# Where a transformer block keeps its modulation sums, which queue writes its spills, and when two modulation sections are loaded

## The chip, the cores and the metric

The kernel runs on one core of a Trainium2 chip. The core has five engines that run side by side and meet through semaphores: TensorE (PE, matmuls), VectorE (DVE), ScalarE (ACT), GpSimd (POOL) and SyncE (SP, which here only issues transfers). Matmuls write to PSUM; everything else lives in SBUF; VectorE and ScalarE can read and write both. Transfers between SBUF and the chip's main memory are issued from an engine's instruction queue and carried by 16 DMA engines. The metric is the device time in microseconds (us) of one execution; lower is better.

## The reference

One transformer block over 1024 tokens of width 1024, in float32, with adaptive layer norm:

```
mod = silu(c) @ w_ada + b_ada                     # 6 sections of 1024
sh_a, sc_a, g_a, sh_f, sc_f, g_f = split(mod, 6)  # sections 0 .. 5
h = rms_norm(x) * (1 + sc_a) + sh_a
x = x + g_a * hybrid_mixer(h, ...)                # w_in, two kinds of attention, w_out
h = rms_norm(x) * (1 + sc_f) + sh_f
x = x + g_f * swiglu(h, w_gate, w_up, w_down)
return rms_norm(x, g_final)
```

The mixer projects `h` by `w_in` (1024 x 2240) into q and k of four "differential" heads (the first 1024 columns), their values dv (512 columns), and two low-rank latents (lq 384, lk 320 columns) from which four further heads (MLA) get their q, k and v by `w_q_up` and `w_kv_up`. Both kinds of attention are causal, in blocks of 128 queries.

The six sections of `mod` are needed at different times. Sections 1 and 0 (scale and shift of the first norm) are needed before the first projection; section 2 (`g_a`) when `w_out` is prepared; 4 and 3 (scale and shift of the second norm) before the feed-forward part; 5 (`g_f`) when `w_down` is prepared, which multiplies it into the weights.

## The kernel before

**Number format.** Every float32 operand of a large matmul is split into two parts, `hi` (rounded by a ScalarE copy) and `lo = raw - hi` (a subtraction on VectorE or GpSimd). `mm3` then issues three matmuls (hi x hi, hi x lo, lo x hi; lines 370 to 372) for each product. The helper `split` does this for weights and activations, `evac` for results that leave PSUM; both subtractions are recorded under line 151.

**Buffers.** Nearly all SBUF tiles, weights, activations and temporaries alike, come from one pool of `NBUF` = 49 slots of 4 KB per partition (`slot`). An instruction that writes a fresh slot waits until the last user of that slot is done; for a tile that is spilled to main memory this last user is the transfer. PSUM has eight banks: two double-bank tiles (`psd`) and four single ones (`psb`).

**Weight streams.** `Stream` is a list of items, each with a load (`dma`) and a preparation (`prep`). `pump(n)` prepares the next n items and keeps `ahead` loads in flight beyond them, but only up to the item named by `allow`; `need(name)` pumps until that item is prepared. All loads are issued on SP's queue, in order. `st` feeds the first half of the kernel, `st2` the weights of `w_out`, gate, up and down.

**Order of the work.** The parts that bear on the change, in program order:

1. `load_ada(k)`, `ada_cols(k)`: scale and shift of the first norm for 128 columns at a time (k = 0 to 7). VectorE multiplies eight 128 x 256 pieces of `w_ada` by the entries of `silu(c)` and adds them up in `acc` (lines 222, 224, 226); TensorE adds over the partitions by four small matmuls against ones (line 229); VectorE writes the two columns `acol` (230, 232). The items `("ada", k)` alternate in `st` with `("s0", k)`, the k-th 128 rows of the q and k weights, whose `lo` part is subtracted on GpSimd.
2. `make_h(hf, k)`: TensorE transposes 128 columns of four normalised x tiles into one PSUM bank (line 356); ScalarE scales and shifts them into the SBUF tile `ht` (361); `split` makes `hh` and `hl` from it.
3. `g1(hf)`, for each half of the tokens: for k = 0 to 7, six targets times `mm3` (18 matmuls of 128 x 512), with `make_h(hf, k + 2)` prepared meanwhile; in the first half, `ada_cols` and the splits of s0 run in this loop. Then the last two targets (48 matmuls). Six targets fill the two `psd` tiles and two of the four `psb` banks. `evac_qk` moves each target into a tile `E` and, some ticks later (`defer`, `tick`), `spill` writes `E` to the scratch arrays `scr_q` and `scr_k` in main memory by two transfers of 256 KB (line 404), issued on GpSimd's queue (`sd`).
4. The dv loop: eight token tiles with 24 matmuls each, evacuated by `evac_v` and spilled by four transfers per pair of tiles (line 472), also on GpSimd's queue.
5. The list `fill`: lq, lk, q_up, kv_up, between which the first units of attention already run; `PUMP` sets how many items of `st` are prepared per entry, `ALLOW` when further items may be loaded.
6. The loop of attention units (`step`), `w_out` and the second norm, gate and up (`gu`), then down.

The other modulation sections are made by `ada_items`: eight loads of 512 KB (`adr`, line 268), each followed by a VectorE multiply-add of 128 x 1024 (lines 275, 277). When the eighth is done, `done` is deferred by three ticks. For `row_bc` (sections 2 and 5) it issues two matmuls against ones (line 299) and two additions; the result `gbc` stays in a slot until it is used. For `col_sec` (sections 4 and 3) it issues eight narrow products (line 309, recorded as 16 matmuls) and the additions into `fcol`. These matmuls are pinned: TensorE executes them where the program text puts them, waiting if the sums aren't there yet. Instructions that are not pinned may be ordered otherwise than in the text when the kernel is built.

The order of `st` before: ada/s0 alternating, x tiles 4 to 7, section 2, section 4, dv, lq, section 3, section 5, lk, rope tables, q_up, kv_up. `g1(1)` may load up to dv; the dv loop up to the end of section 5.

Of the kernel before, what the change touches and what calls it, by code (L numbers as in the profile page):

```python
# [21 lines left out]
LT = 4  # L22
PD = 1
DSP = 2
ALLOW = [(6, 'rope'), (15, ('qup', 2)), (25, ('kvup', 1)), (34, None)]
SPILL = 'gpsimd'
DS = 4
ND = 2
LA = 5
PUMP = (2, 2)  # L30
LC = 1
KEEP = [(n, (0, b)) for n in ("qn", "kn", "qp") for b in range(2)]
LEAD = 2
# [63 lines left out]
def emit(ctx, tc, a, out, dbg=None, rec=None):  # L97
# [21 lines left out]
    def psb():  # L119
        return pp.tile([P, 512], F32, name=nm("psb"), tag="b", bufs=8 - 2 * ND)  # L120
# [93 lines left out]
            ld(out=adar[k][q], in_=a["ada_a"][k, :, q * 4:(q + 1) * 4, :])  # L214

    def ada_cols(k):
        acc = slot([2, 256], F32, "acc")
        for kt in range(8):
            src = adar[k][kt // 4][:, kt % 4, :]
            c = cact[:, kt:kt + 1]  # L220
            if kt < 2:
                nc.vector.tensor_scalar(out=acc[:, kt, :], in0=src, scalar1=c, scalar2=None, op0=ALU.mult)
            else:
                nc.vector.scalar_tensor_tensor(out=acc[:, kt % 2, :], in0=src, scalar=c, in1=acc[:, kt % 2, :],
                                               op0=ALU.mult, op1=ALU.add)
        nc.vector.tensor_tensor(out=acc[:, 0, :], in0=acc[:, 0, :], in1=acc[:, 1, :], op=ALU.add)
        ps = psb()
        for s in range(2):
            mm(ps[:, s:s + 1], lhsT=acc[:, 0, s * 128:(s + 1) * 128], rhs=ones[:, 0:1], start=True, stop=True)
        nc.vector.scalar_tensor_tensor(out=acol[:, 0, k:k + 1], in0=ps[:, 0:1], scalar=b1col(1, k),  # L230
                                       in1=V[:, 56 + k:57 + k], op0=ALU.add, op1=ALU.mult)
        nc.vector.tensor_tensor(out=acol[:, 1, k:k + 1], in0=ps[:, 1:2], in1=bcol(0, k), op=ALU.add)
        del adar[k]
# [3 lines left out]
    def witem(st, name, src, shape, eng=None, split_=None, view=None):  # L237
        def dma():
            raws[name] = slot(shape, F32, "raw")
            ld(out=raws[name], in_=src)  # L240

        def prep():
            hi = slot(shape, F32R, "whi")
            lo = slot(shape, F32R, "wlo")
            split(raws[name], hi, lo, eng)
            W[name] = (hi, lo)
            del raws[name]

        st.add(name, dma, prep)
# [5 lines left out]
    win = a["w_in"]  # L255
    for k in range(8):
        st.add(("ada", k), (lambda k=k: load_ada(k)) if k else (lambda: None), lambda k=k: ada_cols(k))
        witem(st, ("s0", k), win[k * P:(k + 1) * P, 0:1024], [1024], nc.gpsimd)
    for t in range(4, 8):
        st.add(("x", t), lambda t=t: load_x(t), lambda t=t: x_norm(t))  # L260

    accs = {}

    def ada_items(sec, done):
        for kt in range(8):
            def dma(kt=kt):
                raws[("ad", sec, kt)] = slot([1024], F32, "adr")
                ld(out=raws[("ad", sec, kt)], in_=a["w_ada"][kt * P:(kt + 1) * P, sec * 1024:(sec + 1) * 1024])

            def prep(kt=kt):  # L270
                src = raws.pop(("ad", sec, kt))
                c = cact[:, kt:kt + 1]
                if kt == 0:
                    accs[sec] = slot([1024], F32, "acc")
                    nc.vector.tensor_scalar(out=accs[sec], in0=src, scalar1=c, scalar2=None, op0=ALU.mult)
                else:
                    nc.vector.scalar_tensor_tensor(out=accs[sec], in0=src, scalar=c, in1=accs[sec],
                                                   op0=ALU.mult, op1=ALU.add)
                if kt == 7:
                    acc = accs.pop(sec)  # L280
                    defer(3, lambda: done(acc))

            st.add(("ad", sec, kt), dma, prep)

    gbc = {}

    def row_bc(sec):
        def dma():
            raws[("gb", sec)] = slot([1024], F32, "gbr")
            ld(out=raws[("gb", sec)], in_=a["b_ada"][0:1, sec * 1024:(sec + 1) * 1024].to_broadcast([P, 1024]))  # L290

        st.add(("gb", sec), dma, lambda: None)

        def done(acc):
            g = slot([1024], F32, "gbc")
            br = raws.pop(("gb", sec))
            for n in range(2):
                ps = psb()
                pin(mm(ps, lhsT=ones, rhs=acc[:, n * 512:(n + 1) * 512], start=True, stop=True))
                nc.vector.tensor_tensor(out=g[:, n * 512:(n + 1) * 512], in0=ps, in1=br[:, n * 512:(n + 1) * 512], op=ALU.add)  # L300
            gbc[sec] = g

        ada_items(sec, done)

    def col_sec(sec, fin):
        def done(acc):
            ps = psb()
            for j in range(8):
                pin(mm(ps[:, j:j + 1], lhsT=acc[:, j * 128:(j + 1) * 128], rhs=ones[:, 0:1], start=True, stop=True))
            fin(ps)  # L310

        ada_items(sec, done)

    def fin_scf(ps):
        nc.vector.tensor_tensor(out=fcol[:, 0, :], in0=ps[:, 0:8], in1=V1[:, 32:40], op=ALU.add)
# [2 lines left out]
    def fin_shf(ps):  # L318
        nc.vector.tensor_tensor(out=fcol[:, 1, :], in0=ps[:, 0:8], in1=V[:, 32:40], op=ALU.add)

    row_bc(2)
    col_sec(4, fin_scf)
    for q in range(4):
        witem(st, ("dv", q), win[q * 256:(q + 1) * 256, 1024:1536].rearrange("(k p) n -> p k n", p=P), [2, 512], nc.gpsimd)
    for q in range(4):
        witem(st, ("lq", q), win[q * 256:(q + 1) * 256, 1536:1920].rearrange("(k p) n -> p k n", p=P), [2, 384])
    col_sec(3, fin_shf)
    row_bc(5)

    def load_tabs():  # L330
        raws["rope"] = slot([8, 2, 64], F32, "rope")
        ld(out=raws["rope"], in_=a["rope"])

    for q in range(3):
        n = 3 if q < 2 else 2
        witem(st, ("lk", q), win[q * 384:q * 384 + n * 128, 1920:2240].rearrange("(k p) n -> p k n", p=P), [n, 320])
# [2 lines left out]
        witem(st, ("qup", k), a["w_q_up"][k * P:(k + 1) * P, :], [768], nc.gpsimd)  # L339
    for k in range(2):  # L340
        witem(st, ("kvup", k), a["w_kv_up"][k * P:(k + 1) * P, :], [1024], nc.gpsimd)


    def x_norm(t):
# [8 lines left out]
    def make_h(hf, k):  # L353
        ps = psb()
        for t in range(4):
            nc.tensor.transpose(ps[:, t * 128:(t + 1) * 128], xr[hf * 4 + t][:, k * 128:(k + 1) * 128], ident)
        if k % 2 == 0:
            hT[hf, k // 2] = (slot([2, 512], F32R, "hh"), slot([2, 512], F32R, "hl"))
        hi, lo = (z[:, k % 2, :] for z in hT[hf, k // 2])
        tmp = slot([512], F32, "ht")  # L360
        nc.scalar.activation(tmp, ps, AF.Identity, scale=acol[:, 0, k:k + 1], bias=acol[:, 1, k:k + 1])
        split(tmp, hi, lo)

    def h_op(hf, k):
        hi, lo = hT[hf, k // 2]
# [30 lines left out]
    def evac_qk(ps, m, hf):  # L396
        E = slot([2, 512], F32R, "E")
        h = m % 4
        evac(ps, -0.125 / SLOPES[h] if m < 4 else 1.0, E[:, 0, :], E[:, 1, :])

        def spill():
            q = scr["q" if m < 4 else "k"][h, hf].rearrange("(l r) m t -> l m r t", l=2)
            for l in range(2):
                sd(out=q[l], in_=f(E[:, l, :]))

        defer(DS, spill)

# [44 lines left out]
    st.allow(("dv", 3))  # L452
    g1(1)
    st.need(("dv", 3))
    st.allow(("ad", 5, 7))


    vt = {}
# [1 line left out]
    def evac_v(ps, name, t):  # L460
        if t % 2 == 0:
            vt[name] = (slot([2, 512], F32R, "vh"), slot([2, 512], F32R, "vl"))
        hi, lo = vt[name]
        evac(ps, 1.0, hi[:, t % 2, :], lo[:, t % 2, :])
        if t % 2 == 0:
            return

        def spill():
            for l, z in ((0, hi), (1, lo)):
                for tt in range(2):  # L470
                    u = t - 1 + tt
                    sd(out=scr[name][:, u // 4, :, l, u % 4, :].rearrange("h p d -> p h d"),
                       in_=f(z[:, tt, :]).rearrange("p (h d) -> p h d", h=4))

        defer(DS, spill)
# [225 lines left out]
    NP = NF // 2  # L701
    KINDS = ("gate", "up")
    scratch("g", [NF, P, 1024])
    for c in range(NP):
        its = [it for kind in KINDS for it in ops_items(kind, c)]
        for z in IT0 if c == 0 else range(8):
            st2.add(*its[z])
    for fi in range(NF):
        down_item(fi)
        g_item(fi)  # L710
# [574 lines left out]
```

## Time and profile before

| | before |
|---|---|
| median of 3 runs (lowest to highest) | 1356.33 us (1353.53 to 1357.04) |
| the profiled execution | 1355.32 us |
| its span, first to last instruction | 1353.5 us |
| mean granted TensorE clock | 0.965 |
| TensorE matmuls busy | 1245.5 us, 92% of the span |
| VectorE busy | 843.7 us, 62% |
| GpSimd busy | 534.8 us, 40% |
| ScalarE busy | 454.7 us, 34% |
| bytes moved by DMA | 180.61 MB |

In the rows of the profile an instruction is named by its line, engine, operation and tiles ("out<-in"); numbers of buffers are left out, so that `hl<-ht,hh` stands for every subtraction that makes an `hl`. A matmul's record is longer than the time after which the next one starts: matmuls overlap, and the rate is read from how many start in a stretch. "[9.24 <-DVE hl L151]" behind a row means that the engine was idle for 9.24 us before it and what ended that. Rows of waits give the engine that waited, what it waited for, the total, the times and the longest. Rows of transfers give what is issued, from which queue, how often, the size of one and the median time from issue to landing; those of queues, packets, MB and the share of the 16 DMA engines. `PEclk` is the clock that TensorE was granted, 1.00 being the full one.

### The profile page before, as it was taken

What the parts mean: (1) busy time and instruction counts of PE and PEld (TensorE: products, weight loads), DVE (VectorE), ACT (ScalarE), POOL (GpSimd) and SP (SyncE); (2) the same over time, 40 slices, a digit from 0 to 9 for tenths busy, and PEclk for the clock granted to TensorE, in tenths of its full rate; (3) what the DMA queues carried; (4) which work ended last, traced back from release to release, by engine and by line L of the source; (5) the groups of instructions that cost most, each with busy time, mean ns of one, the idle gap of its engine ahead of it and who ended that gap; (6) DMA issues with size and microseconds to landing.
All of it is one profiled execution on the core that took longest, in us unless ns stands there. A gap on an engine that the chain in (4) does not pass through costs nothing.

```text
span 1353.5 us, 16478 instructions
## 1 busy us (share of the span) xinstructions
PE 1245.5 (92%) x6033; PEld 1041.0 (77%) x6033; DVE 843.7 (62%) x1219; ACT 454.7 (34%) x801; POOL 534.8 (40%) x576
## 2 busy tenths in 40 slices
PE   4795995999999999999889999999999988999996
PEld 3574774898888898887668888888888866887885
DVE  6762426165778887867875545565555689576446
ACT  3241220254566676314632232322232332121002
POOL 3341421236564335412474444455544563221003
PEclk9897896999999999999999999999999989999998
DMA  9537589433687533441021222222221764231003
GB/s 365 198 73 192 184 189 330 141 118 98 214 293 255 172 114 108 154 140 62 32 84 57 94 94 87 84 88 85 93 70 55 247 267 134 68 125 47 0 0 124
DMA packets 66765, 180.61 MB, mean 133 GB/s; under 512 B 20654, under 2 KB 23036, under 8 KB 66556
## 3 DMA queue, kind: packets, MB, share of 16 engines
q1 hardware_dynamic: 40891, 139.58, 30.0%
q0 software_dynamic: 25792, 39.97, 10.1%
q8 instruction: 48, 0.79, 0.2%
q14 instruction: 34, 0.27, 0.1%
HBM read 135.37 MB, written 44.04 MB: 133 GB/s over the span
## 4 chain that ended last, share of the span: by engine, by line
PE 70%; DVE 11%; DMA 7%; issue 5%; ACT 4%; POOL 2%; SPq 0%; POOLq 0%; DVEq 0%; ACTq 0%
PE psb L370 14%; PE psb L371 14%; PE psb L372 14%; PE psd L371 6%; PE psd L370 5%; PE psd L372 5%; PE psb L829 2%; DMA adr<-in_w_ada_dram 2%; DMA scr_q<-E 2%; DMA scr_k<-E 1%; DVE x L1175 1%; DVE wlo L151 1%; PE psb L853 1%; PE psb L854 1%; PE psb L852 1%
## 5 line engine op out<-in xcount | busy, mean ns | idle before, releaser
L371 PE MATMUL psb<-al,whi 128*128 128x512 f32 x528 | 206.8, 392 | 3.5 <-DVE al L151 3.5
L370 PE MATMUL psb<-ah,whi 128*128 128x512 f32 x528 | 206.6, 391 | 0.2 <-ACT ht L1057 0.2
L372 PE MATMUL psb<-ah,wlo 128*128 128x512 f32 x528 | 206.2, 391 | 0.0
L1175 DVE TENSOR_TENSOR x<-psd,x 128x1024 f32<-128x1024 f32 x87 | 105.8, 1220 | 77.5 <-PE psd L372 77.5
L370 PE MATMUL psd<-dhi,whi 128*128 128x512 f32 x348 | 138.1, 397 | 13.0 <-DVE x L1175 12.9
L371 PE MATMUL psd<-dlo,whi 128*128 128x512 f32 x348 | 136.8, 393 | 0.0
L372 PE MATMUL psd<-dhi,wlo 128*128 128x512 f32 x348 | 136.8, 393 | 0.0
L1134 DVE TENSOR_TENSOR cf<-psb,uv 128x512 f32<-128x512 f32 x88 | 60.4, 686 | 115.7 <-PE psb L372 115.1
L1141 POOL TENSOR_TENSOR cf<-cf,cf 128x512 f32<-128x512 f32 x44 | 61.7, 1402 | 178.9 <-DVE cf L1134 173.6
L371 PEld LDWEIGHTS psb<-al,whi 128*128 128x128 f32 x528 | 99.5, 188 | 25.2 <-DVE al L151 4.7
L370 PEld LDWEIGHTS psb<-ah,whi 128*128 128x128 f32 x528 | 99.7, 189 | 21.7 <-ACT ht L1057 0.7
L372 PEld LDWEIGHTS psb<-ah,wlo 128*128 128x128 f32 x528 | 99.6, 189 | 20.8
L639 POOL TENSOR_TENSOR raw<-raw,gbc 128x1024 f32<-128x1024 f32 x26 | 66.9, 2587 | 102.9 <-DVE x L1175 48.8
L151 DVE TENSOR_TENSOR wlo<-raw,whi 128x1024 fp32r<-128x1024 f32 (+3 forms) x51 | 92.7, 1823 | 6.4 <-ACT whi L155 5.0
L155 ACT CAST whi<-ssum 128x1024 fp32r<-128x1024 f32 x44 | 45.0, 1044 | 136.2 <-POOL ssum L151 136.2
L370 PEld LDWEIGHTS psd<-dhi,whi 128*128 128x128 f32 x348 | 66.0, 190 | 30.8 <-DVE x L1175 17.2
L151 DVE TENSOR_TENSOR wlo<-ssum,whi 128x1024 fp32r<-128x1024 f32 x44 | 62.9, 1430 | 39.5 <-ACT whi L155 39.5
L748 ACT ACTIVATE s<-s,nb 128x640 f32<-128x640 f32 (+7 forms) x96 | 74.5, 778 | 34.0 <-DVE nb L746 30.6
L746 DVE CUSTOM_DVE_ANT_0 s<-psd,tabs 128x640 f32<-128x640 f32 (+7 forms) x80 | 63.4, 804 | 32.2 <-PE psd L772 30.3
L155 ACT CAST whi<-raw 128x1024 fp32r<-128x1024 f32 (+3 forms) x68 | 68.5, 1019 | 41.9 <-DVE dlo L151 29.9
L372 PEld LDWEIGHTS psd<-dhi,wlo 128*128 128x128 f32 x348 | 66.0, 190 | 14.2 <-DVE wlo L151 0.3
L371 PEld LDWEIGHTS psd<-dlo,whi 128*128 128x128 f32 x348 | 66.2, 190 | 13.6
(290 smaller groups left out, 2958.5 us busy)
## 6 DMA issues: line engine op xcount, KB each, us to landing
adr<-in_w_ada_dram SPq DMA_DIRECT2D x32, 512.0 KB, 10.5
raw<-in_w_gate_dram SPq DMA_DIRECT2D x22, 512.0 KB, 4.4
raw<-in_w_up_dram SPq DMA_DIRECT2D x22, 512.0 KB, 3.4
scr_g<-cf POOLq DMA_DIRECT2D x22, 512.0 KB, 4.4
raw<-in_w_down_dram SPq DMA_DIRECT2D x22, 512.0 KB, 4.3
raw<-scr_g SPq DMA_DIRECT2D x22, 512.0 KB, 4.6
ada<-in_ada_a_dram SPq DMA_DIRECT2D x16, 512.0 KB, 10.2
x<-in_x_dram SPq DMA_DIRECT2D x16, 512.0 KB, 5.1
```

The lines of the kernel that those rows point to most:

```text
L151: eng.tensor_tensor(out=o, in0=x, in1=y, op=ALU.subtract)
L155: nc.scalar.copy(hi, raw)
L370: mm(o, lhsT=ah, rhs=bh, start=start, stop=False)
L371: mm(o, lhsT=ah, rhs=bl, start=False, stop=False)
L372: mm(o, lhsT=al, rhs=bh, start=False, stop=stop)
L639: eng.tensor_tensor(out=r, in0=r, in1=gbc[sec], op=ALU.mult)
L746: nc.vector.tensor_tensor_reduce(out=s, in0=src, in1=tab, op0=ALU.add, op1=ALU.min, scale=scale, scalar=3.0e38, accum_out=nb[:, m:m + 1])
L748: nc.scalar.activation(s, s, AF.Exp, bias=nb[:, m:m + 1], scale=-1.0, accum_out=rs[:, m:m + 1])
L829: nc.tensor.transpose(ps[:, z * 128:(z + 1) * 128], p[:, kb * 128:(kb + 1) * 128], ident)
L1134: nc.vector.tensor_tensor(out=o, in0=x, in1=y, op=ALU.add)
L1141: nc.gpsimd.tensor_tensor(out=g, in0=g, in1=o, op=ALU.mult)
L1175: nc.vector.tensor_tensor(out=r, in0=d.rearrange("p a b -> p (a b)"), in1=r, op=ALU.add)
```

## The change

Four things are changed.

- `ada_cols` takes a PSUM bank at its start and keeps its two running sums in it; only the eighth product goes to an SBUF tile, to which the other sum is added. The column sums then go to the same bank.
- `make_h` writes the scaled and shifted block back to the PSUM bank of the transposes; the slot `ht` goes. The `lo` part of `s0,0` is subtracted on VectorE.
- The spills of q, k and dv are issued on ScalarE's queue, those of the MLA heads stay on GpSimd's.
- Section 3 leaves `st` for a stream `st3` that is pumped once per attention step after the list `fill`; section 5 joins `st2`, two items behind each gate/up pair from the second on, and a `tick` is added to the gate/up loop; section 4 goes behind dv, its load of `b_ada` (`gb`) of section 2 two items later. The limits are set anew: the dv loop may load up to lk, `ALLOW` has three entries, `PUMP` is one item per entry.

```diff
-ALLOW = [(6, 'rope'), (15, ('qup', 2)), (25, ('kvup', 1)), (34, None)]
+ALLOW = [(0, 'rope'), (12, ('qup', 2)), (25, None)]
-PUMP = (2, 2)
+PUMP = (1, 1)
     def ada_cols(k):
-        acc = slot([2, 256], F32, "acc")
+        ps = psb()
+        part = [ps[:, 0:256], ps[:, 256:512]]
+        acc = slot([256], F32, "acc")
         for kt in range(8):
             src = adar[k][kt // 4][:, kt % 4, :]
             c = cact[:, kt:kt + 1]
             if kt < 2:
-                nc.vector.tensor_scalar(out=acc[:, kt, :], in0=src, scalar1=c, ...)
+                nc.vector.tensor_scalar(out=part[kt], in0=src, scalar1=c, ...)
             else:
-                nc.vector.scalar_tensor_tensor(out=acc[:, kt % 2, :], in0=src, scalar=c, in1=acc[:, kt % 2, :],
+                nc.vector.scalar_tensor_tensor(out=acc if kt == 7 else part[kt % 2], in0=src, scalar=c, in1=part[kt % 2],
                                                op0=ALU.mult, op1=ALU.add)
-        nc.vector.tensor_tensor(out=acc[:, 0, :], in0=acc[:, 0, :], in1=acc[:, 1, :], op=ALU.add)
-        ps = psb()
+        nc.vector.tensor_tensor(out=acc, in0=acc, in1=part[0], op=ALU.add)
...
-        witem(st, ("s0", k), win[k * P:(k + 1) * P, 0:1024], [1024], nc.gpsimd)
+        witem(st, ("s0", k), win[k * P:(k + 1) * P, 0:1024], [1024], nc.gpsimd if k else nc.vector)
...
-    row_bc(2)
-    col_sec(4, fin_scf)
-    # dv, lq
-    col_sec(3, fin_shf)
-    row_bc(5)
+    for it in row_bc(2):
+        st.add(*it)
+    # dv
+    for it in col_sec(4, fin_scf):
+        st.add(*it)
+    # lq, lk, rope, qup, kvup
+    st3 = Stream(2)
+    for it in col_sec(3, fin_shf):
+        st3.add(*it)
...
-        tmp = slot([512], F32, "ht")
-        nc.scalar.activation(tmp, ps, AF.Identity, scale=acol[:, 0, k:k + 1], bias=acol[:, 1, k:k + 1])
-        split(tmp, hi, lo)
+        nc.scalar.activation(ps, ps, AF.Identity, scale=acol[:, 0, k:k + 1], bias=acol[:, 1, k:k + 1])
+        split(ps, hi, lo)
...
-                sd(out=q[l], in_=f(E[:, l, :]))
+                nc.scalar.dma_start(out=q[l], in_=f(E[:, l, :]))
...
-    st.allow(("ad", 5, 7))
+    st.allow(("lk", 2))
...
-                    sd(out=scr[name][:, u // 4, :, l, u % 4, :].rearrange("h p d -> p h d"),
+                    (nc.scalar.dma_start if name == "dv" else sd)(out=scr[name][:, u // 4, :, l, u % 4, :].rearrange("h p d -> p h d"),
...
+    late_ada = row_bc(5)
     for c in range(NP):
...
+        if c >= 1:
+            for _ in range(2):
+                if late_ada:
+                    st2.add(*late_ada.pop(0))
...
         step(n, LA)
+        if n > done:
+            st3.allow()
+            st3.pump()
...
             next(gen[w])
             more(m)
+            tick()
```

More of the change, by code (lines that the diff above doesn't have):

```diff
@@ L221, in ada_cols @@
             if kt < 2:
-                nc.vector.tensor_scalar(out=acc[:, kt, :], in0=src, scalar1=c, scalar2=None, op0=ALU.mult)
+                nc.vector.tensor_scalar(out=part[kt], in0=src, scalar1=c, scalar2=None, op0=ALU.mult)
             else:
-                nc.vector.scalar_tensor_tensor(out=acc[:, kt % 2, :], in0=src, scalar=c, in1=acc[:, kt % 2, :],
+                nc.vector.scalar_tensor_tensor(out=acc if kt == 7 else part[kt % 2], in0=src, scalar=c, in1=part[kt % 2],
                                                op0=ALU.mult, op1=ALU.add)
-        nc.vector.tensor_tensor(out=acc[:, 0, :], in0=acc[:, 0, :], in1=acc[:, 1, :], op=ALU.add)
-        ps = psb()
+        nc.vector.tensor_tensor(out=acc, in0=acc, in1=part[0], op=ALU.add)
         for s in range(2):
-            mm(ps[:, s:s + 1], lhsT=acc[:, 0, s * 128:(s + 1) * 128], rhs=ones[:, 0:1], start=True, stop=True)
+            mm(ps[:, s:s + 1], lhsT=acc[:, s * 128:(s + 1) * 128], rhs=ones[:, 0:1], start=True, stop=True)
         nc.vector.scalar_tensor_tensor(out=acol[:, 0, k:k + 1], in0=ps[:, 0:1], scalar=b1col(1, k),
@@ L264, in ada_items @@
     def ada_items(sec, done):
+        its = []
         for kt in range(8):
@@ L281, in prep @@
                     defer(3, lambda: done(acc))
-            st.add(("ad", sec, kt), dma, prep)
+            its.append((("ad", sec, kt), dma, prep))
+        return its
     gbc = {}
@@ L290, in dma @@
             ld(out=raws[("gb", sec)], in_=a["b_ada"][0:1, sec * 1024:(sec + 1) * 1024].to_broadcast([P, 1024]))
-        st.add(("gb", sec), dma, lambda: None)
         def done(acc):
@@ L301, in done @@
             gbc[sec] = g
-        ada_items(sec, done)
+        its = ada_items(sec, done)
+        return its[:6] + [(("gb", sec), dma, lambda: None)] + its[6:]
     def col_sec(sec, fin):
@@ L310, in done @@
             fin(ps)
-        ada_items(sec, done)
+        return ada_items(sec, done)
     def fin_scf(ps):
@@ L319, in fin_shf @@
         nc.vector.tensor_tensor(out=fcol[:, 1, :], in0=ps[:, 0:8], in1=V[:, 32:40], op=ALU.add)
-    row_bc(2)
-    col_sec(4, fin_scf)
[L323 to L326, printed above, removed]
-    col_sec(3, fin_shf)
-    row_bc(5)
     def load_tabs():
@@ L332, in load_tabs @@
         ld(out=raws["rope"], in_=a["rope"])
+    for it in row_bc(2):
+        st.add(*it)
+    for q in range(4):
+        witem(st, ("dv", q), win[q * 256:(q + 1) * 256, 1024:1536].rearrange("(k p) n -> p k n", p=P), [2, 512], nc.gpsimd)
+    for it in col_sec(4, fin_scf):
+        st.add(*it)
+    for q in range(4):
+        witem(st, ("lq", q), win[q * 256:(q + 1) * 256, 1536:1920].rearrange("(k p) n -> p k n", p=P), [2, 384])
     for q in range(3):
```

## The prediction

> **What bounds the kernel now.** I read the windows by stage first, then the waits of TensorE, then the engines' timelines where it waited.
>
> ```profile
> 20.00:95.30 75.30, 63.08 (x248) 48.61 (x249) 56.30 (x99) 23.93 (x37) 29.47 (x23) 0.86 0.52 184
> 95.30:171.50 76.20, 58.35 (x236) 45.88 (x235) 26.02 (x31) 18.39 (x27) 22.92 (x21) 0.82 0.67 186
> 171.50:245.20 73.70, 55.26 (x223) 44.58 (x223) 31.49 (x40) 10.43 (x17) 16.90 (x22) 0.84 0.90 273
> 420.00:580.00 160.00, 156.01 (x1031) 140.19 (x1029) 128.73 (x293) 93.79 (x208) 66.66 (x95) 1.00 0.45 145
> 700.00:1000.00 300.00, 300.00 (x1325) 248.53 (x1324) 163.75 (x173) 83.98 (x111) 152.00 (x112) 1.00 0.24 85
> ```
>
> Each row gives a stretch and its length, the busy time (and number) of TensorE's matmuls, its weight loads, VectorE, ScalarE and GpSimd, then TensorE's granted clock, the DMA share and GB/s. The first three rows are `g1(0)`, `g1(1)` and the dv loop; then attention; last, gate/up. In gate/up TensorE does 1325 matmuls in 300 us, 0.226 us each, never idle, at full clock. The first three stages each hold 192 matmuls of that width, 43.4 us of work, and take 74 to 76 us, with the granted clock down to 0.82-0.86. The change works there, so what it can win is there. What ended TensorE's waits before 400 us (total, times, longest):
>
> ```profile
> PE psd L371 <- DVE hl L151: 18.0, 6, 9.2
> PE psb L309 <- DVE acc L277: 16.1, 1, 16.1
> PE psb L229 <- DVE acc L226: 13.6, 5, 8.3
> ```
>
> **g1(0): VectorE stands still while GpSimd subtracts.**
>
> ```profile
> 15.16 2.34 POOL L151 TENSOR_TENSOR wlo<-raw,whi 128x1024 fp32r<-128x1024 f32 x1
> 15.23 2.82 DVE L349 TENSOR_SCALAR x<-x,rstd 128x1024 f32<-128x1024 f32 x1 [0.71 <-POOL rstd L204]
> 21.07 2.45 POOL L151 TENSOR_TENSOR wlo<-raw,whi 128x1024 fp32r<-128x1024 f32 x1 [3.57 <-ACT whi L155]
> 6.63 2.46 DVE L224 SCALAR_TENSOR_TENSOR acc<-ada,cact,acc 128x256 f32<-128x256 f32 x6
> 21.21 4.57 DVE L224 SCALAR_TENSOR_TENSOR acc<-ada,cact,acc 128x256 f32<-128x256 f32 x6
> 29.70 2.81 DVE L151 TENSOR_TENSOR hl<-ht,hh 128x512 fp32r<-128x512 f32 x1
> 36.09 0.69 DVE L151 TENSOR_TENSOR hl<-ht,hh 128x512 fp32r<-128x512 f32 x1 [1.67 <-ACT hh L155]
> 149.03 9.48 POOL L151 TENSOR_TENSOR wlo<-raw,whi 128x1024 fp32r<-128x1024 f32 x4 [28.39 <-ACT whi L155]
> 154.01 1.29 DVE L394 SCALAR_TENSOR_TENSOR E<-psd,E 128x512 fp32r<-128x512 f32 x2 [0.66 <-ACT E L393]
> ```
>
> Six accumulations take 2.46 us alone and 4.57 us beside a GpSimd subtraction; `hl` takes 0.69 us or 2.81 us. The delayed operations have all their operands in SBUF. Each collision costs 2.1 us, and the last pair of rows shows what escapes it: while GpSimd runs four subtractions in a row, two VectorE operations with a PSUM operand take 0.65 us each, undisturbed. The change gives a PSUM operand to just the operations that collide in the loop: all nine of `ada_cols`, and `hl` (now from `ps`).
>
> The price of a step k, new. VectorE, one after the other:
>
> ```profile
> 27.14 0.61 DVE L222 TENSOR_SCALAR acc<-ada,cact 128x256 f32<-128x256 f32 x2
> 25.82 0.43 DVE L226 TENSOR_TENSOR acc<-acc 128x256 f32<-128x256 f32 x1
> 26.30 0.61 PE L229 MATMUL psb<-ones,acc 128*128 128x1 f32 x4 [1.53 <-DVE acc L226]
> 26.77 0.64 PE L356 MATMUL psb<-ident,x 128*128 128x128 f32 x4
> 26.94 0.22 DVE L230 SCALAR_TENSOR_TENSOR acol<-psb,V,V 128x1 f32<-128x1 f32 x1 [0.70 <-PE psb L229]
> 27.08 0.15 DVE L232 TENSOR_TENSOR acol<-psb,V 128x1 f32<-128x1 f32 x1
> 20.10 0.80 PE L370 MATMUL psd<-hh,whi 128*128 128x512 f32 x1 [1.52 <-ACT hh L155]
> 95.30 1.03 PE L356 MATMUL psb<-ident,x 128*128 128x128 f32 x8
> ```
>
> 0.61 + 2.46 + 0.43 + 0.37 (`acol`) + 0.69 (`hl`) = 4.6 us. TensorE: 18 x 0.226 + about 0.9 (column sums and transposes, start to start) = 5.0 us. Now a step takes (95.3 - 20.1 - 48 x 0.226)/8 = 8.0 us. New wait: the accumulators hold a PSUM bank, and of the four `psb` banks two are targets of the projection. So `ada_cols(k+1)` starts only when `acol(k)` has freed its bank; the chain accumulate, column sum (0.61), `acol`, `hl` is then 5.2 us, plus TensorE's queue in front of the column sums. I take **6.0 us**, the chain with 0.8 us of queueing behind three or four matmuls. What writing PSUM from VectorE or ScalarE costs no row shows. Below: a step at TensorE's 5.0 us. Above: each of the eight accumulations as dear as a 512-wide 0.69 instead of 0.41, +2.2 us, which is today's 8 us; I stay near the row that is closest in kind, the 512-wide pair, which costs the same from PSUM (0.65) as from SBUF (0.69). The two opening multiplications may go from 0.31 to the 0.41 of an accumulation; that 0.2 us is inside the 0.8. With the collisions gone, what is late next is this hand-over through TensorE. Splitting `s0,0` on VectorE spares the norm at 15.23 its 2.1 us; the split itself, about 1.3 us by the 1024-wide `L277` below, lies beside the transposes and ScalarE's work on the first `h`. So the first matmul comes at 18. Stage end: 18 + 48 + 10.8 = 77 instead of 95.3: **-18** (bounds -26 and -2).
>
> [...]
>
> **g1(1): slots held by spills.**
>
> ```profile
> 122.01 0.79 PE L371 MATMUL psd<-hl,whi 128*128 128x512 f32 x1 [9.24 <-DVE hl L151]
> 134.74 0.80 PE L371 MATMUL psd<-hl,whi 128*128 128x512 f32 x1 [5.14 <-DVE hl L151]
> DVE hl L151 <- DMA scr_k<-E: 12.0, 1, 12.0
> POOL scr_k L404 <- DMA scr_q<-E: 31.4, 12, 8.4
> q0 software_dynamic: 8448, 4.25, 42.6%
> q1 hardware_dynamic: 1167, 4.26, 24.1%
> scr_q<-E POOLq DMA_DIRECT2D x16, 256.0 KB, 17.6
> op<-scr_q SPq DMA_DIRECT2D x32, 256.0 KB, 4.8
> ```
>
> `hl` waits for a slot that an `E` holds until its spill has landed; GpSimd cannot issue the next spill before an earlier one landed. The two queue rows are of 84 to 136 us: 4.25 MB of spills cost 42.6% of the DMA time, the same bytes of loads 24.1%, packets of 0.5 KB against 3.7 KB. The change moves the 48 q, k and dv spills to ScalarE's queue, takes the eight `ad4` loads (4 MB) out of this stage, and needs no `ht` slot. Work: 43.4 + 4.1 (32 transposes by the row of eight above) + 3.0 (`L299`) = 50.5 us; 2.5 us is `L309`, which goes to dv; 23 us are stalls and the half clock after them. I keep a third, 8 us, since slots still run out: 16 s0, 16 h, 8 E, 4 x are 44 of 49 before dv's weights come. **-17** (bounds -26: no stall; -2: all of it).
>
> A spill is emitted four ticks after its evacuation, so the half that VectorE writes is normally done when ScalarE reaches the issue; were it not, the next `ht` or evacuation would queue behind it (rival 5). ScalarE pays for 48 issues, 0.34 us each by SP's row below (0.80 each on GpSimd): 16 to 38 us, where it is busy 18.4 of 76 and 10.4 of 74 us; that is covered, and GpSimd, which loses 48 x 0.8 = 38 us, bounds nothing here, so it counts as 0 on both sides.
>
> **dv: the pinned sum of ad3.**
>
> ```profile
> 221.12 3.58 PE L309 MATMUL psb<-ones,acc 128*128 128x1 f32 x16 [16.05 <-DVE acc L277]
> SPq L618 <- PE psb L299: 22.2, 1, 22.2
> L268 SPq DMA_DIRECT2D adr<-in_w_ada_dram x32: 327/338/5296, 58.0 to 220.9; - x32
> adr<-in_w_ada_dram SPq DMA_DIRECT2D x32, 512.0 KB, 10.5
> L277 DVE SCALAR_TENSOR_TENSOR acc<-adr,cact,acc x28: 1274/1285/1286, 90.0 to 236.0; 128x1024 f32<-128x1024 f32 x28
> 243.37 1.88 PE L299 MATMUL psb<-acc,ones 128*128 128x512 f32 x4
> ```
>
> TensorE stood 16 us before ad3's column sums: its loads came late, because SP's queue stood 22.2 us at `lam` for a slot. In their place comes ad4 alone: eight loads in two batches of 10.5 us, 21 us; its sums stand, by the pump's four items a tile and the three ticks of `defer`, behind the fourth of eight dv tiles, 4 x 24 x 0.226 = 22 us in. On SP they stand ahead of lq's and lk's loads, which are needed only after dv, 20 us later. That is close, so I leave a stall of 8: 43.4 + 2.5 + 8 = 54 instead of 73.7 us: **-20** (bounds -28: no stall; -2: the stall stays and only `L299` leaves).
>
> **What comes back later.** ad3 lands in attention: about 0.75 + 7 x 1.29 = 9.8 us of VectorE, which is busy 129 of 160 us, and 2.5 us of `L309`. SP gets eight loads of 0.5 MB among the operands of attention, at a DMA share of 0.45, and three slots are held for it, one of which is the `gbc` of section 5 that no longer waits there. TensorE is busy 156 of 160 us, so what VectorE is late by shows at once: I take `L309` and a quarter of VectorE's time, +5 (bounds +2.5: only `L309`; +12: all of it). ad5 lands in gate/up, where VectorE is busy 164 of 300 us: hidden, but TensorE never idles there, so `L299` costs its 1.9 us: +2 (up to +12 if the cover fails). lk's weights move up into dv, the other preparations of the fill are spread thinner (PUMP), all under its full TensorE: 0. Sum **+7**.
>
> 1355.3 (the profiled execution: span 1353.5 and 1.8 around it) - 18 - 17 - 20 + 7 = 1307.3. The median lies 1.0 above that execution: **1308 us**.
>
> **Rivals.**
>
> 1. *Spills land as late.* By what the queue rows show, DMA time may bind, not GpSimd's issue. Then g1(1) gains 2, not 17: 1323. For it: 0.5 KB packets may be due to the address pattern. Against: 31.4 us of GpSimd waiting. [...]
> 2. *The two banks serialise `ada_cols` and `make_h`*, and a step stays at 8 us: 1308 + 16 = 1324.
> 3. *The late sections are not covered*: 24 instead of 7: 1325. Two of these three together: about 1338.
> 4. *TensorE alone binds the first three stages*: the lower bounds, -26 - 26 - 28 + 4.5, give about 1280.
> 5. *ScalarE's queue is blocked, slower.* A spill waiting on ScalarE for an earlier transfer holds up `ht`, `hh` and the evacuations behind it, and through them TensorE. GpSimd waits thus today:
>
> ```profile
> POOL scr_dv L472 <- DMA scr_k<-E: 8.4, 2, 7.3
> ```
>
> With 31.4 that is about 40 us. If ScalarE took them all uncovered and g1(1) and dv gained nothing: 1308 + 17 + 20 + 40 = 1385. It decides once a wait outlasts TensorE's stock of two steps, 36 x 0.226 = 8.1 us; the longest now is 8.4.
>
> **How the numbers follow.** Forecast 0.47, 1281-1318 by itself; rivals 1, 2, 3: 0.12, 0.08, 0.10; two together 0.05; rival 4 0.10; rival 5 0.06; gains and losses cancelling 0.02. The range runs from 1280 to 1338: below it half of rival 4, above it rival 5, no change and part of the pairs. A measurement of this kernel tells about 0.3% (4 us) from no change: faster 0.92, within 0.02, slower 0.06.
>
> **What would show it.** `hl` and the sums of ada near 0.69 and 0.41 us beside GpSimd's subtractions; the first transposes of `g1(1)` near 77 us; `g1(1)` without waits of 5 us and more; spills on ScalarE landing in under 10 us; no 16 us wait before `L309`; attention longer by some 5 us. Wrong would make it: ScalarE idle on transfers ahead of `ht` or `vh`, column sums waiting several us each step, or TensorE idle in gate/up.

## The result, and the profile after

| | before | after |
|---|---|---|
| median (lowest to highest) | 1354.93 us of 4 runs (1350.61 to 1357.04) | 1427.05 us of 4 runs (1425.35 to 1430.1) |
| ratio after / before, with 95% interval | | 1.0539 (1.0505 to 1.0573) |
| span of the profiled execution | 1353.5 us | 1423.6 us |
| mean granted TensorE clock | 0.965 | 0.946 |

The change makes the kernel 5.4% slower. The forecast was 1308 us, in a range of 1280 to 1338. To see where the time came from, cut both spans at the same events: the first transposes of `g1(1)`, the first matmul of `lq`, the second norm's transposes, the start of gate/up and the start of the down projection. The windows of before with these cuts:

```profile
95.30:173.60 78.30, 60.45 (x245) 47.59 (x244) 26.79 (x33) 18.73 (x27) 24.09 (x23) 0.83 0.68 185
173.60:244.70 71.10, 52.66 (x214) 42.60 (x212) 30.22 (x37) 10.08 (x16) 15.24 (x21) 0.83 0.90 277
244.70:646.80 402.10, 392.23 (x2387) 348.85 (x2385) 283.57 (x633) 204.93 (x471) 167.30 (x302) 1.00 0.46 150
646.80:1084.40 437.60, 428.29 (x1884) 352.18 (x1882) 259.05 (x260) 139.31 (x181) 228.68 (x157) 0.99 0.26 92
```

and of after (columns as in the prediction: stretch and length, matmuls, weight loads, VectorE, ScalarE, GpSimd, granted clock, DMA share, GB/s):

```profile
20.00:82.00 62.00, 55.27 (x244) 42.51 (x243) 44.27 (x92) 21.87 (x33) 21.76 (x15) 1.00 0.53 204
82.00:209.20 127.20, 57.69 (x230) 44.69 (x229) 18.12 (x24) 19.55 (x30) 9.50 (x4) 0.70 0.25 87
209.20:306.80 97.60, 51.98 (x209) 42.53 (x208) 22.27 (x31) 11.73 (x17) 0.00 (x0) 0.74 0.48 154
306.80:712.80 406.00, 395.40 (x2401) 351.21 (x2401) 288.31 (x637) 202.90 (x469) 169.92 (x300) 1.00 0.49 160
712.80:1153.40 440.60, 429.53 (x1888) 351.68 (x1887) 270.21 (x270) 138.88 (x181) 232.68 (x157) 1.00 0.30 102
```

The first stage became shorter: `g1(0)` ends at 82.0 instead of 95.3 us and now runs at full clock. Everything lost is in the next two rows. `g1(1)` and dv together take 224.9 us (82.0 to 306.85, the first matmul of `lq`) instead of 149.4. TensorE does about the same work in them (109.7 against 113.1 us busy), the granted clock is down to 0.70 and 0.74, and the DMA share of `g1(1)` is 0.25 where it was 0.68. So the transfers moved less data per microsecond than before (87 against 185 GB/s), while TensorE waited. The sum of the stages: -13.3 + 75.5 + 8.0 (attention, gate/up and the end) = +70.2, and the spans differ by 70.1.

What ended TensorE's waits between 82 and 306 us (total, times, longest):

```profile
PE psd L373 <- ACT hh L155: 55.2, 2, 30.9
PE psb L373 <- DVE E L151: 31.1, 2, 19.4
PE psb L311 <- DVE acc L279: 26.2, 1, 26.2
```

The largest is ScalarE's `hh`. What did ScalarE do? The rows of the two places that spill (duration of an issue in ns, min/median/max; first and last start):

```profile
L407 ACTq DMA_DIRECT2D scr_q<-E x16: 495/4772/5015, 72.4 to 204.9; - x16
L407 ACTq DMA_DIRECT2D scr_k<-E x16: 3354/6196/7512, 103.1 to 249.7; - x16
```

```profile
L475 ACTq DMA_DIRECT2D scr_dv<-vh x8: 366/367/7098, 258.3 to 307.7; - x8
```

An issue of a q or k spill holds ScalarE's sequencer for 4.8 or 6.2 us at the median, one of a dv spill, on the same queue, for 0.37 us. ScalarE's timeline (start, length, how many issues in a row; in brackets, idle time and what ended it) shows what stands behind them:

```profile
72.44 1.06 ACTq L407 DMA_DIRECT2D scr_q<-E  x1
78.00 4.75 ACTq L407 DMA_DIRECT2D scr_q<-E  x1
82.87 9.98 ACTq L407 DMA_DIRECT2D scr_q<-E  x2
92.90 0.58 ACT L393 CAST E<-psb 128x512 fp32r<-128x512 f32 x1 [9.52 <-issue]
118.75 31.43 ACTq L407 DMA_DIRECT2D scr_k<-E  x5
150.28 0.75 ACT L364 ACTIVATE psb<-psb,acol 128x512 f32<-128x512 f32 x1 [34.15 <-DMA adr<-in_w_ada_dram]
```

The early issues are short. From 78 us on nearly every one takes 3.4 to 7.5 us, about what one transfer takes (5.1 us, below), as if the queue were full and emptied one transfer at a time; how many it holds no row shows. An evacuation (0.58 us) waited 9.5 us behind two of them. At 118.75 five issues in a row took 31.4 us, and the activation that makes the next `h` came behind them. Its wait is put down to a load of `adr`, which is what came last; its own queue's row, directly above, says that the engine stood in its issues for 31.4 of these 34.2 us. The rows of all 32 issues in that timeline add up to 148 us. TensorE then waited for that activation:

```profile
151.70 0.79 PE L373 MATMUL psd<-hh,whi 128*128 128x512 f32 x1 [24.32 <-ACT hh L155]
```

The waits for `E` came the same way: the evacuation at 243.7 us, which ended the longest of them, stood behind six issues of 33.7 us. Together `hh` and `E` are 86 of the 112 us in the first three rows of TensorE's waits.

Why does an issue take 5 us? The queue rows of after, 81 to 112 us (packets, MB, share of the 16 DMA engines; the mean rate in that stretch is 51 GB/s):

```profile
q10 hardware_dynamic: 781, 1.57, 13.1%
```

For 31 us nearly nothing else moves, several spills are queued, and the share never leaves 13%, which is about 2 engines of 16. Counted from the start and length of each packet in the trace, two data packets are under way for 27.7 of these 31 us. A spill of 256 KB at 51 GB/s takes 5.1 us, the 16 of one half of the tokens in sequence 82 us; ScalarE's two blocks of issues last 78 us (72.4 to 150.2) and 76 us (179.9 to 256.2).

There is a second chain. An `E` slot is held until its spill has landed, so the loads that need a slot come late. What SP's queue waited for (0 to 400 us):

```profile
SPq L270 <- DMA scr_k<-E: 139.3, 11, 70.2
```

That is why ad4's column sums (`L311` above) kept TensorE waiting 26.2 us, though ad3 had been moved out of their way.

### The profile page after: what moved, and what is told of

Read it like the earlier page. It is cut to its first block, busy times and chain, and to the rows that moved or that the text cites. A ratio compares the mean times of both kernels' runs of the same rounds, so it can differ in the third digit from the quotient of the medians.

```text
span 1423.6 us, 16415 instructions
## 1 busy us (share of the span) xinstructions
PE 1242.2 (87%) x6033; PEld 1036.3 (73%) x6033; DVE 833.6 (59%) x1220; ACT 453.3 (32%) x801; POOL 503.6 (35%) x527
## 4 chain that ended last, share of the span: by engine, by line
PE 63%; DVE 8%; DMA 6%; issue 3%; ACT 2%; ACTq 2%; POOL 1%; SPq 0%; POOLq 0%; DVEq 0%
PE psb L373 13%; PE psb L375 13%; PE psb L374 13%; PE psd L373 5%; PE psd L374 5%; PE psd L375 5%; DMA scr_k<-E 3%; PE psb L837 2%; DVE x L1186 1%; ACTq L407 1%; DMA adr<-in_w_ada_dram 1%; DMA op<-scr_q 1%; PE psb L861 1%; PE psb L862 1%; DVE wlo L151 1%
## 5 line engine op out<-in xcount | busy, mean ns | idle before, releaser
L1152 POOL TENSOR_TENSOR cf<-cf,cf 128x512 f32<-128x512 f32 x44 | 65.6, 1492 | 178.9 <-DVE cf L1145 173.4
L151 DVE TENSOR_TENSOR wlo<-raw,whi 128x1024 fp32r<-128x1024 f32 (+3 forms) x52 | 89.6, 1730 | 1.8 <-POOL raw L642 1.2
L373 PE MATMUL psb<-whi,hh 128*128 128x512 f32 (+2 forms) x192 | 68.9, 359 | 19.6 <-DVE E L151 19.4
L151 POOL TENSOR_TENSOR wlo<-raw,whi 128x1024 fp32r<-128x1024 f32 (+1 forms) x16 | 37.3, 2334 | 125.7 <-ACT whi L155 116.8
```

Source lines behind the costliest of these rows:

```text
L151: eng.tensor_tensor(out=o, in0=x, in1=y, op=ALU.subtract)
L373: mm(o, lhsT=ah, rhs=bh, start=start, stop=False)
L1152: nc.gpsimd.tensor_tensor(out=g, in0=g, in1=o, op=ALU.mult)
```

## The experiments

The first theory was that the pattern of the q and k spills is at fault. The scratch is written as `q[l]` = (m, r, t), sizes 2 x 64 x 512: its slowest dimension is 2, while that of a dv spill is 128. I read the 13.1% above as two DMA engines, one for each of the two blocks; if that is so, the spills queued behind a transfer wait for it, and any hardware queue would suffer. The rivals: the PSUM part or the new order of loads costs the time; or ScalarE is simply the wrong engine for spills, whatever their pattern. The results together (ratio to the kernel before, measured beside it; "after" and "before" name what was edited):

| label | edit | median us | ratio (95% interval) |
|---|---|---|---|
| a_split | after; each q/k spill cut in two | 1309.49 | 0.9684 (0.9654 to 0.9715) |
| b_qk_pool | after; q/k spills back on GpSimd | 1330.77 | 0.9844 (0.9805 to 0.9883) |
| c_before_qk_act | before; only q/k spills to ScalarE | 1438.33 | 1.0636 (1.0597 to 1.0676) |
| h_qk_sp | after; q/k spills on SP | 1427.94 | 1.0566 (1.0531 to 1.06) |
| e_psum | before; only the PSUM part | 1333.91 | 0.9846 (0.9808 to 0.9884) |
| d_before_split | before; spills to ScalarE, q/k cut | 1321.42 | 0.9759 (0.972 to 0.9797) |
| f_order | before; only the new load order | 1355.24 | 1.0007 (0.9984 to 1.0029) |
| j_layout | after; scratch laid out (m r) l t | 1310.0 | 0.9668 (0.9634 to 0.9702) |
| k_psum_split | before; PSUM part and d's spills | 1307.19 | 0.966 (0.9637 to 0.9683) |
| l_two_queues | k; only q on ScalarE | 1308.49 | 0.9665 (0.964 to 0.9689) |
| i_split_pool | after; q/k cut, on GpSimd | 1299.21 | 0.9608 (0.958 to 0.9635) |
| m_dose | k; six extra transfers at the end | 1357.05 | one run |

**a_split: the pattern, repaired.** The bytes, the queue and the program order stay; each spill becomes two of 64 partitions each, so that the slowest dimension of either is 64.

```diff
-                nc.scalar.dma_start(out=q[l], in_=f(E[:, l, :]))
+                for m_ in range(2):
+                    nc.scalar.dma_start(out=q[l][m_], in_=f(E[m_ * 64:(m_ + 1) * 64, l, :]))
```

> The changed kernel with each q or k spill of 128 partitions cut into two of 64, so that the slowest dimension of the target is 64 and not 2. Theory (the pattern 2 x 64 x 512 runs on 2 of the 16 DMA engines, 51 GB/s, and ScalarE stands about 5 us at each issue): issues take about 0.37 us, spills land in under 10 us, no wait for hh or E of more than 5 us, and the whole takes about 1313 us (1355 - 13 - 17 - 20 + 8). Rival (ScalarE's queue stands because spills and SP's loads wait for one another, whatever the pattern): twice the issues, no better, 1400 us or more.

It took 1309.49 us, 8% less than the changed kernel, by nothing but the cut. Its spills, by source line, and the landing of all of them:

```profile
L408 ACTq DMA_DIRECT2D scr_q<-E x32: 452/607/760, 73.5 to 137.0; - x32
L408 ACTq DMA_DIRECT2D scr_k<-E x32: 452/607/1610, 86.5 to 155.4; - x32
...
DMA to landing us min/median/max: 2.2/2.4/7.4
```

Twice as many issues cost 64 x 0.61 = 39 us of ScalarE instead of 148, and they land in 2.4 us. Its windows:

```profile
83.10:142.70 59.60, 51.81 (x229) 41.11 (x228) 17.44 (x23) 19.16 (x29) 9.47 (x4) 0.94 0.69 198
142.70:188.10 45.40, 45.40 (x209) 37.78 (x209) 22.38 (x31) 11.75 (x17) 0.00 (x0) 1.00 0.93 296
188.10:596.10 408.00, 396.07 (x2402) 351.51 (x2400) 288.62 (x637) 203.32 (x469) 170.28 (x300) 1.00 0.48 159
596.10:1036.00 439.90, 429.58 (x1887) 351.59 (x1885) 269.74 (x270) 138.90 (x181) 232.83 (x157) 1.00 0.30 102
```

`g1(1)` takes 59.6 us and dv 45.4, in which TensorE never idles, where the change as made took 127 and 98. So the pattern alone, repaired, takes the whole loss back.

**c_before_qk_act: the suspected cause alone.** The kernel before, with only the q and k spills put on ScalarE's queue.

```diff
-                sd(out=q[l], in_=f(E[:, l, :]))
+                nc.scalar.dma_start(out=q[l], in_=f(E[:, l, :]))
```

> The kernel before with only the q and k spills on ScalarE. Theory of the pattern: the same 5 us per issue and 51 GB/s, so 32 x 5.2 = 166 us of ScalarE's queue in two blocks, of which some 80 to 90 us are not covered: about 1440 us. Rival (the loss needs the new order of the loads): within 1345 to 1370 us.

1438.33 us, as expected: this one line alone costs 6.4%, and the other parts of the change win some of it back. The issues cost what they cost in after:

```profile
L404 ACTq DMA_DIRECT2D scr_q<-E x16: 500/4756/5008, 85.6 to 221.4; - x16
```

**h_qk_sp: another hardware queue, the same pattern.**

```diff
-                nc.scalar.dma_start(out=q[l], in_=f(E[:, l, :]))
+                ld(out=q[l], in_=f(E[:, l, :]))
```

> The changed kernel with the q and k spills issued on SP, pattern unchanged. Theory of the pattern: the transfers still run on 2 engines at about 51 GB/s, SP's queue stands about 5 us at each and the loads behind them come late, while ScalarE is free: about 1400 us, DMA share about 0.13 while only spills run. Rival (something of ScalarE's own queue): issues of 0.34 us as for SP's loads, landing under 10 us, 1320 us or less.

1427.94 us: with ScalarE free of every q and k issue the time is that of after. I had expected about 28 us less, because ScalarE would no longer stand. SP's queue stands instead, and the loads behind it are late. The issues, the queue row (85 to 110 us), then the waits (75 to 300 us):

```profile
L407 SPq DMA_DIRECT2D scr_q<-E x16: 486/4171/7154, 73.2 to 213.9; - x16
```

```profile
q1 hardware_dynamic: 634, 1.28, 13.1%
```

```profile
DVE acc L279 <- DMA adr<-in_w_ada_dram: 79.1, 3, 67.4
...
PE psb L311 <- DVE acc L279: 62.7, 1, 62.7
```

The same 13.1% on another queue. So it isn't ScalarE: given this pattern, either queue, ScalarE's (after) or SP's (here), drains at 51 GB/s, and whoever issues it stands: q and k issues take 4.8 and 6.2 us at the median on ScalarE, 4.2 and 4.9 on SP. That the two times are equal is partly luck, for TensorE waits for other things here (62.7 us for the sums above and 62.1 us for an `hl`, but only 1.6 us for `hh`).

**b_qk_pool: the pattern kept, back on GpSimd** (`sd(...)` in place of `nc.scalar.dma_start(...)`; dv stays on ScalarE).

> The changed kernel with q and k spilled on GpSimd again, dv still on ScalarE. Both theories: ScalarE never stands at an issue. If the rest of the change is worth what was forecast, with the old slow landing of the spills (about 20 us) left in the second half, about 1325 us; if the rest of the change loses too (loads placed wrongly, sections in attention), 1355 us or more.

1330.77 us, 0.4% above the expectation. GpSimd carries the same pattern without ruin; its queue from 75 to 160 us:

```profile
DMA packets 16659, 11.86 MB, mean 140 GB/s; under 512 B 13349, under 2 KB 13435, under 8 KB 16526
q0 software_dynamic: 15035, 7.53, 49.7%
```

One transfer in this pattern is no faster there (m_dose, below), but several run beside each other: by the packets' records mostly four to ten data packets are under way at once (56 of the 70 us in which there is one), where the hardware queue had two. The mean of 0.5 KB a packet (7.53 MB / 15035) hides two kinds: 1812 data packets of 4 KB, and 13223 packets of 4 or 8 bytes, which take 208 of the 676 us that the queue's packets take in all.

**i_split_pool: the same with the spills cut in two** (`sd(...)` in a_split's edit).

> The changed kernel with q and k cut into two of 64 partitions but spilled on GpSimd. Theory (the 0.5 KB packets and the 20 us to landing come from the pattern there too): packets of 2 KB, landing under 10 us, about 1312 us. Rival (they come from GpSimd's queue): packets of 0.5 KB, 1325 to 1335 us as with whole spills.

1299.21 us, the fastest of all, and below both what I expected (1312) and the rival. Its spills on GpSimd:

```profile
DMA to landing us min/median/max: 2.3/5.8/7.1
```

```profile
q0 software_dynamic: 2686, 7.34, 33.1%
```

Nearly the same bytes go in 2686 packets instead of 15035: 1792 data packets of 4 KB, about as many as before, and 894 of 4 bytes; those of 8 bytes are gone. The packets take 344 us of the engines' time (33.1% of 16 over 65 us) instead of 676 (49.7% over 85 us). Against b_qk_pool only the pattern differs, and the ratio falls by 0.024, some 31 us. That GpSimd is the better queue by 10 us against a_split I had not foreseen; the 39 us of issues that ScalarE no longer pays are the likely reason, but no run takes them away by themselves, so it stays argued.

**j_layout: another cure.** The scratch of q and k is laid out as (m r) l t, so an `E` goes in one transfer of 512 KB with 128 rows; k is loaded in two halves.

```diff
-            for l in range(2):
-                nc.scalar.dma_start(out=q[l], in_=f(E[:, l, :]))
+            nc.scalar.dma_start(out=scr["q" if m < 4 else "k"][h, hf], in_=f(E))
```

> The changed kernel with q and k laid out in main memory as the tile lies in SBUF (partition, half, token): one spill of 512 KB for each tile, slowest dimension 128, and the loads of k cut into two of 64 partitions. Theory: 16 engines, 16 issues on ScalarE in place of 64 for q and k, so some of the 14 us go that evacuations waited behind issues in the version cut in two (1309 us): 1300 to 1310 us. Rival (the loads in attention suffer from more and smaller transfers): 1315 us or more.

1310.0 us. dv is over at 182.0 instead of 188.1, but the rest of the span takes 1125.6 us instead of a_split's 1117.8: what is won early comes back later, perhaps because each k tile now needs two loads, which no run separates. Two different cures of the pattern end within 1 us of each other.

**e_psum, d_before_split, f_order: the parts one by one**, each alone on the kernel before. e_psum takes the diffs of `ada_cols`, `make_h` and `s0,0`; d_before_split only the spills, as in a_split and with dv on ScalarE; f_order only the order of loads with `ALLOW` and `PUMP`.

> The kernel before with only the PSUM part (sums of ada and scaled h in PSUM, lo of s0,0 on VectorE). Theory (stages add up): the first half's stage is shorter by the 13 us that it was in the changed kernel, and nothing later is touched: about 1339 us. Rival (the gain is swallowed by the second half, which then waits that much longer for slots): 1350 us or more.

> The kernel before with the q, k and dv spills on ScalarE, q and k cut into two of 64 partitions. Theory: with spills that land in 2 to 8 us the waits for slots in the second half (14 us, and the half clock behind them) go, and section 3 in the dv loop is loaded earlier: about 1325 to 1335 us. Rival (the queue matters little where the pattern is right): 1350 us.

> The kernel before with only the new order of the loads (sections 3 and 5 late, 4 behind dv, ALLOW and PUMP); sums in SBUF, all spills on GpSimd. Theory: from the changed kernel with q and k on GpSimd (1331 us) and the 13 us of the PSUM part, about 1340 us. Rival (the late sections cost as much as the early stages gain): 1352 us or more.

e_psum wins 1.5%, d_before_split 2.4%, a little more than expected each. What dv's move to ScalarE is worth by itself no run shows. f_order missed: I had expected about 15 us of gain, and it makes no measurable difference. By its stages the first three win 6.2 us (`lq` begins at 238.5 instead of 244.7) and the rest gives back 9.8 (1118.6 against 1108.8 us); the profiled span, of one execution each, is 3.6 us longer. What was to go away is still there (waits of 80 to 260 us):

```profile
PE psb L310 <- DVE acc L278: 17.9, 1, 17.9
```

TensorE waits 17.9 us for the pinned column sums as it did 16.1 before, only that they are ad4's now. In both orders, with the spills as in before, the section whose sums stand in the dv loop is late; with d_before_split's spills, in the old order, the wait is 0.2 us.

**k_psum_split: without the order.** The PSUM part and d's spills on the kernel before.

> The kernel before with the PSUM part and with the q, k and dv spills on ScalarE, q and k cut into two; the order of the loads as before. Theory (the new order wins nothing once the spills land fast, and costs 9 us in attention and gate/up): the early stages end near 192 us, the rest takes 1109 to 1112 us: about 1303 us, a few us below the version with the new order (1309). Rival (the new order is what keeps the dv loop free of waits): 1315 us or more, with a wait before section 3's column sums.

1307.19 us, 4 above the expectation. The ratios of k and a_split overlap, so the order of loads makes no measurable difference with cured spills either. e's and d's gains, 1.5% and 2.4%, give 3.9% if they add up; k has 3.4%, so the two parts share a little.

**l_two_queues: half of the spills each.** As k, with q on ScalarE and k and dv on GpSimd, q and k cut.

> As the run before, but only q is spilled on ScalarE (cut in two); k (cut in two) and dv go on GpSimd. Theory (what is left in the second half are evacuations behind issues on ScalarE): 1295 to 1303 us. Rival (GpSimd's spills land late whatever the cut): 1310 to 1325 us, with waits for slots in the second half.

1308.49 us, a miss: no better than k. TensorE's longest wait for `hh` is 10.0 us where k's is 6.5. Why two queues don't help here, while GpSimd for both q and k helps in i_split_pool (in the new order of loads), is open.

**m_dose: the pattern by itself.** At the end of k_psum_split one tile of 512 KB is written six times to a scratch, one after the other, with the slowest dimension set to 2, 4, 8 and 16 on SP's queue and to 2 and 16 on GpSimd's. Its time includes these transfers.

```diff
+    for eng, k_ in ((nc.sync, 2), (nc.sync, 4), (nc.sync, 8), (nc.sync, 16), (nc.gpsimd, 2), (nc.gpsimd, 16)):
+        eng.dma_start(out=z_[0:128 + k_].rearrange("(k r) d -> k r d", k=k_)[:, 0:128 // k_, :], in_=o_)
```

> The kernel of the first of these four runs, with six transfers of the same 512 KB tile to a scratch array added behind the end, each waiting for the one before: from SP with targets of 2 x 64, 4 x 32, 8 x 16 and 16 x 8 rows (a gap behind each block), then from GpSimd with 2 x 64 and 16 x 8. Theory (a transfer from a hardware queue gets as many DMA engines as the slowest dimension counts): 51, 102, 204 and about 330 to 400 GB/s, that is 10, 5, 2.6 and 1.4 us of transfer, each with some 2 us of latency. Rival (only the access order matters, not the count): the four alike. From GpSimd no difference in engines is expected; the packets may differ.

The chain that ended last, for the four on SP (start, length):

```profile
1301.22 13.02 DMA scr_z<-oz
...
1314.30 10.02 DMA scr_z<-oz
...
1324.34 5.90 DMA scr_z<-oz
...
1330.26 3.73 DMA scr_z<-oz
```

The same bytes take 13.0, 10.0, 5.9 and 3.7 us with 2, 4, 8 and 16 blocks. By the packets' records 2, 4, 8 and 16 packets are under way at a time through most of the four transfers, one for each block, as the theory said. The time doesn't halve with each doubling all the same: a packet of 4 KB takes 0.18 us with two under way and 0.23 to 0.24 us with four or more, and each transfer takes about 1.5 us besides. So 4 blocks took 10.0 us, where I had expected 7. GpSimd's two, by their windows' rows (first 2 blocks, then 16):

```profile
DMA packets 1040, 0.53 MB, mean 38 GB/s; under 512 B 912, under 2 KB 912, under 8 KB 1040
q0 software_dynamic: 1040, 0.53, 13.3%
```

```profile
q0 software_dynamic: 144, 0.52, 26.8%
```

They landed after 13.4 and 3.6 us. So a single transfer of two blocks is as slow on GpSimd as on SP. Its data go in 128 packets of 4 KB, two at a time, as on SP; the other 912 of its packets are small ones. GpSimd's advantage in b_qk_pool is only that it has several transfers under way at once.

## Why the prediction was wrong

**The step that failed** is one sentence of the working: "ScalarE pays for 48 issues, 0.34 us each by SP's row below (0.80 each on GpSimd): 16 to 38 us ... that is covered, and GpSimd ... bounds nothing here, so it counts as 0 on both sides." The row it rested on was that of `adr` loads, whose slowest dimension is 128. For the 16 dv spills it is right (0.37 us). For the 32 q and k spills an issue took about as long as one transfer at 51 GB/s (5.1 us), 4.8 and 6.2 us at the median: 148 us of ScalarE instead of some 11, in front of `h` and the evacuations. A second choice failed with it: that the spills would land sooner because GpSimd no longer holds them back. They drain one after the other at 51 GB/s, where GpSimd's queue in the same stage of before moved 4.25 MB in 52 us (84 to 136 us), 82 GB/s. Of the two this pace is the root: h_qk_sp spares ScalarE every issue of q and k and takes as long. How the loss divides between the engine that stands and the slots that are held, no run separates. Two rows pointed there and weren't followed: the 0.5 KB packets, which rival 1 put down to "the address pattern" without asking what that pattern would do on another queue; and the maximum of 5.296 us in the very row of issues, of which only the median was used. The 0.5 KB were also misread: they are a mean over 1024 data packets of 4 KB and 7424 of 4 or 8 bytes, so the spills' data went in packets as large as the loads'.

What the pattern does is measured: 13.1% of 16 engines with two blocks on ScalarE's queue (after) and on SP's (h_qk_sp), and 2, 4, 8 and 16 packets at a time with as many blocks in m_dose. On GpSimd's queue several such transfers ran beside each other (49.7% in b_qk_pool), on the hardware queues they did not; why, and which engines they used, the traces don't tell.

**Rival 5 had the place and not the cause.** "ScalarE's queue is blocked" is what happened, and through `hh` and the evacuations as it said. But it took the waits from GpSimd's (40 us), as if ScalarE would wait for what GpSimd waited for. It gave 1385 and a chance of 0.06; the measured 1427 is 42 above even that, for the blocked queue also held the slots and so delayed `adr` (SP's queue waited 139.3 us for spills of k).

**g1(0), -18 forecast, -13.3 measured.** The mechanism was right. VectorE's groups in the first 100 us of before:

```profile
L224 DVE SCALAR_TENSOR_TENSOR acc<-ada,cact,acc 128x256 f32<-128x256 f32 x48 | 28.4, 653 | 0.0
L151 DVE TENSOR_TENSOR hl<-ht,hh 128x512 fp32r<-128x512 f32 x10 | 13.2, 1323 | 9.4 <-ACT hh L155 9.4
L222 DVE TENSOR_SCALAR acc<-ada,cact 128x256 f32<-128x256 f32 x16 | 4.9, 347 | 1.9 <-DMA ada<-in_ada_a_dram 1.9
```

and in the first 90 us of after (busy us, mean ns of one):

```profile
L226 DVE SCALAR_TENSOR_TENSOR psb<-ada,cact,psb 128x256 f32<-128x256 f32 x40 | 19.5, 488 | 1.2
L224 DVE TENSOR_SCALAR psb<-ada,cact 128x256 f32<-128x256 f32 x16 | 7.8, 486 | 2.6 <-DMA ada<-in_ada_a_dram 2.2
...
L151 DVE TENSOR_TENSOR hl<-psb,hh 128x512 fp32r<-128x512 f32 x8 | 5.5, 687 | 1.5 <-ACT hh L155 1.5
```

The collisions are gone: `hl` fell from a mean of 1.32 us to 0.69, the sums from 0.65 to 0.49. But an undisturbed accumulation took 0.41 in SBUF and takes 0.49 in PSUM, and an opening multiplication 0.49 instead of 0.31. Per step that is 5 x 0.08 + 2 x 0.18 = 0.8 us more VectorE time than I had taken. A step came out at (82.0 - 19.05 - 10.8)/8 = 6.5 us instead of 6.0, which is 4 us in eight, and the first matmul at 19.05 instead of 18. I had gone by the 512-wide rows. They hold (0.687 from PSUM against 0.69 from SBUF), and the 256-wide accumulations are 0.08 us dearer all the same. The nearest row in kind was not near enough.

**g1(1) and dv, -17 and -20 forecast, +75.5 measured together.** With the pattern cured (a_split) they give 59.6 and 45.4 us instead of 78.3 and 71.1, -18.7 and -25.7. So the stalls were what the prediction said, and they go if the spills do land sooner. But the 16 us wait for the pinned sums goes with the spills, not with the order of loads: f_order kept it, and d_before_split, in the old order, waits 0.2 us there. The term's size was near and its reason wrong, which is luck.

**What comes back later, +7 forecast, +8.0 measured** (attention +3.9, gate/up +3.0, the rest 1.1), and 9.0 in a_split, 9.8 in f_order. Right in kind and size. Together with the last point it makes the order of loads worth nothing: it pays this and gains only what cured spills give anyway.

The total of 1308 would have been right for a_split (1309.49), with two errors of opposite sign in it: `g1(0)` 6 too good (-18 against -12.2), the two stages after it 7 too poor (-37 against -44.4). For the change as made, it is 119 us off, and the cut of the spills alone takes 118 of them back. A small slip in the sums: two of the first three rivals together give 1339 to 1341, not 1338.

## What to carry to other kernels

Before a transfer is moved from GpSimd to a hardware queue, look at the slowest dimension of the pattern it writes: here, with 2, it ran at 51 GB/s and most issues held the engine for about 5 us, and cutting it into two transfers of 64 cured it (issues of 0.61 us, landing in 2.4). Take the price of an issue from a row with the same pattern, not from another transfer on the same kind of queue, and read the maximum beside the median. Time the parts of a bundled change one by one: here one part won 1.5%, one nothing, and the third, the spills, lost 6.4% as written (q and k alone) and won 2.4% when its pattern was mended.

## What the hardware showed that was not expected

The engine that issues paid for the spills that were still queued: the first took ScalarE 0.5 to 1.8 us to issue, those behind them mostly about 5 us, and up to 7.5. The queue's pace went with the pattern (13.0 us for 512 KB with 2 blocks, 3.7 with 16), and was the same on ScalarE's and SP's queues: 13.1% of the DMA engines, 51 GB/s. On GpSimd one such transfer of 512 KB took 13.4 us, as on SP (13.0), and needed 1040 packets for 128 of data, but several in flight reached 49.7% of the engines. And VectorE's 256-wide sums with target and source in PSUM cost 0.49 us where they cost 0.41 in SBUF, while a 512-wide subtraction cost 0.69 from either.
